# Top-2 expert dispatch: an early store of one row per partition instead of three, and the first group's other four stores with 16 rows each

## The chip, the cores and the metric

The kernel runs on one core of a Trainium2 chip. The metric is the device time of one execution in microseconds; lower is better. The time of the kernel before is the median of three runs. A profiled execution, taken by the hardware profiler, supplies the trace.

## What is computed

```python
batch, seq, hidden, n_experts, k = 16, 1024, 512, 8, 2
...
probs = softmax(router_logits)                       # over the 8 experts
topk_indices = np.argsort(probs, axis=-1)[..., -k:]
topk_probs = np.take_along_axis(probs, topk_indices, axis=-1)
topk_probs = topk_probs / np.sum(topk_probs, axis=-1, keepdims=True)
x_expanded = x[:, :, np.newaxis, :].repeat(k, axis=2)
return (x_expanded * topk_probs[..., np.newaxis]).astype(np.float32)
```

(The first two lines of the softmax are written as one call here.) For each of 16,384 tokens the two largest of 8 router probabilities are scaled to sum to one, and the token's 512 values are written out twice, once times each of the two weights, the smaller first. The output has 67.1 MB, twice the 33.6 MB of `x`.

## The kernel before

**Tiling.** The tokens are cut into two groups. Group 0 has 65 tokens per partition, group 1 has 63, on 128 partitions. A "row" is one token on each partition: 2 KB of `x` per partition going in, 4 KB per partition (two scaled copies) going out. Each group lies so that a partition's tokens are contiguous in memory, so that a load or store of n rows moves one contiguous run per partition.

**Buffers.** `xs` holds 65 rows of `x`. `osp` holds `L = 18` rows of output. There is no room for a whole group of outputs, so half of the stores write their products into `osp`, and the other half write them into parts of `xs` whose input rows are no longer needed (an output row takes two rows of `xs`).

**Loads.** `LOADS` gives the rows of each load: 2, 4, 28 and 31 for group 0, and 16, 16 and 31 for group 1. All are issued by SP at line 122. After the first six rows the two router-logit transfers are issued (lines 130 and 131) and `top2_weights` computes all weights into `WA`: a tournament of maxima and minima on VectorE (lines 26 to 36) and two sigmoids on ScalarE (lines 37 and 38). Its scratch lies in `osp`.

**Stores.** `STORES` lists each store as (first row, rows, buffer, place in the buffer). For each, VectorE multiplies the rows of `xs` with the weights into the place (line 138), then the store is issued (line 151). The very first store of group 0, the early store, is issued by ACT; the rest are issued by SP in program order, after the loads that stand ahead of them in the code. In group 0 these are:

```python
[(0, 3, "osp", 0), (3, 15, "osp", 3), (18, 16, "xs", 0), (34, 15, "osp", 0), (49, 16, "xs", 33)],
```

In this document they are called the early store, store 1, store 2, the third store (store 3) and store 4. Group 1 has four stores of 16, 16, 15 and 16 rows.

**Splitting the third store's product.** A product that goes to place 0 of `osp` again is cut in two (`again`, line numbers just above 138): the first `FREE[g]` rows lie where the early store's rows lay, and need only that store to have landed. The rest lie where store 1's rows lay and need store 1 to have landed. `FREE` is 3 for group 0 and 2 for group 1.

**Order of the work.** Transfers on SP go out in the order of the code: the group's loads, then its stores, then the next group's loads. The scheduler places VectorE's instructions. The loads of group 1 write rows of `xs` that stores 2 and 4 of group 0 read, and wait for these to land; the last, of 31 rows, waits for store 4.

Of the kernel before, what the change touches and what calls it, by code (L numbers as in the profile page):

```python
# [1 line left out]

# [4 lines left out]

F32 = mybir.dt.float32
ALU = mybir.AluOpType
ACTF = mybir.ActivationFunctionType  # L10
P = 128


def top2_weights(nc, WA, dlt, room, logits, E):

    tt = nc.vector.tensor_tensor
    hi, lo, n = None, None, E  # L20
    while n > 1:
        n //= 2
        if hi is None:
            a, b = logits[:, :, 0:n], logits[:, :, n : 2 * n]
            nhi, nlo = room(n), b
            tt(nhi, a, b, op=ALU.max)  # L26
            tt(nlo, a, b, op=ALU.min)  # L27
        else:
            a, b = hi[:, :, 0:n], hi[:, :, n : 2 * n]
            nhi, nlo, tmp = room(n), room(n), room(n)  # L30
            tt(tmp, lo[:, :, 0:n], lo[:, :, n : 2 * n], op=ALU.max)  # L31
            tt(nlo, a, b, op=ALU.min)  # L32
            tt(nlo, nlo, tmp, op=ALU.max)  # L33
            tt(nhi, a, b, op=ALU.max)  # L34
        hi, lo = nhi, nlo
    tt(dlt, hi[:, :, 0], lo[:, :, 0], op=ALU.subtract)  # L36
    nc.scalar.activation(WA[:, :, 0], dlt, ACTF.Sigmoid, scale=-1.0)  # L37
    return nc.scalar.activation(WA[:, :, 1], dlt, ACTF.Sigmoid, scale=1.0)  # L38

GROUPS = [65, 63]

LOADS = [[2, 4, 28, 31], [16, 16, 31]]
BASE = [0, 1]

STORES = [
    [(0, 3, "osp", 0), (3, 15, "osp", 3), (18, 16, "xs", 0), (34, 15, "osp", 0), (49, 16, "xs", 33)],
    [(0, 16, "osp", 2), (16, 16, "xs", 0), (32, 15, "osp", 0), (47, 16, "xs", 32)],
]  # L50

L = 18

FREE = [3, 2]


@with_exitstack
def kernel(
    ctx: ExitStack,
    tc: tile.TileContext,  # L60
    x: bass.AP,
    router_logits: bass.AP,
    k: bass.AP,
    out: bass.AP,
):
    nc = tc.nc
    B, S, D = x.shape
    E = router_logits.shape[-1]
    N = B * S
    assert int(k) == 2 and E == 8 and N == P * sum(GROUPS)  # L70
    M = N // P

    x_v, o_v, rl_v = [], [], []
    t0 = 0
    for n in GROUPS:
        t1 = t0 + P * n
        x_v.append(
            x.rearrange("b s d -> (b s) d")[t0:t1].rearrange("(p m) d -> p m d", p=P)
        )
        o_v.append(  # L80
            out.rearrange("b s k d -> (b s) k d")[t0:t1].rearrange(
                "(p m) k d -> p m k d", p=P
            )
        )
        rl_v.append(
            router_logits.rearrange("b s e -> (b s) e")[t0:t1].rearrange(
                "(p m) e -> p m e", p=P
            )
        )
        t0 = t1  # L90

    wpool = ctx.enter_context(tc.tile_pool(name="wpool", bufs=1))
    xs = wpool.tile([P, max(GROUPS), D], F32)
    osp = wpool.tile([P, L, 2, D], F32)
    WA = wpool.tile([P, M, 2], F32)
    dlt = wpool.tile([P, M], F32)


    flat = osp.rearrange("p l k d -> p (l k d)")
    taken = [0]  # L100

    def room(n):
        o = taken[0]
        taken[0] += M * n
        return flat[:, o : o + M * n].rearrange("p (m n) -> p m n", n=n)

    logits = room(E)

    def place(where, at, n):

        if where == "osp":
            return osp[:, at : at + n]
        return xs[:, at : at + 2 * n, :].rearrange("p (r k) d -> p r k d", k=2)

    moved = []
    m0 = 0
    for g, G in enumerate(GROUPS):
        x0, r = BASE[g], 0
        for n in LOADS[g]:
            moved.append(  # L120
                tc.keep_in_program_order(
                    nc.sync.dma_start(  # L122
                        xs[:, x0 + r : x0 + r + n, :], x_v[g][:, r : r + n, :]
                    )
                )
            )
            r += n
            if g == 0 and r == 6:
                n0 = GROUPS[0]
                tc.keep_in_program_order(nc.sync.dma_start(logits[:, :n0], rl_v[0]))  # L130
                tc.keep_in_program_order(nc.sync.dma_start(logits[:, n0:], rl_v[1]))  # L131
                weights = top2_weights(nc, WA, dlt, room, logits, E)
        assert r == G
        for r, n, where, at in STORES[g]:
            og = place(where, at, n)
            again = where == "osp" and at == 0 and r > 0
            for a, b in [(0, FREE[g]), (FREE[g], n)] if again else [(0, n)]:
                product = nc.vector.tensor_tensor(  # L138
                    og[:, a:b],
                    xs[:, x0 + r + a : x0 + r + b, :]  # L140
                    .unsqueeze(2)
                    .to_broadcast([P, b - a, 2, D]),
                    WA[:, m0 + r + a : m0 + r + b, :]
                    .unsqueeze(3)
                    .to_broadcast([P, b - a, 2, D]),
                    op=ALU.mult,
                )

            queue = nc.scalar if g == r == 0 else nc.sync
            moved.append(  # L150
                tc.keep_in_program_order(queue.dma_start(o_v[g][:, r : r + n], og))  # L151
            )
        m0 += G

    seen = tc.keep_in_program_order(nc.sync.nop())
    for ins in [weights, product] + moved[:-1]:
        tc.add_manual_dep(
            seen.ins,
            ins.ins.name,
            mybir.DependencyInfo(  # L160
                mybir.DependencyClass.Sync, mybir.DependencyReason.DATA
            ),
            reason="all but the last transfer is done",
        )


# [1 line left out]
_INS = ['x', 'router_logits', 'k']  # L168
_OUTS = [((16, 1024, 2, 512), 'float32')]

_NUMBERS = {'k': 2}


# [26 lines left out]
```

## Time and profile before

| what | us |
|---|---|
| median of the three runs | 239.71 (239.63 to 239.90) |
| the profiled execution, its own time | 241.36 |
| its span, first to last instruction | 239.6 |
| VectorE busy | 141.9, 22 instructions |
| ScalarE busy | 1.8 |
| VectorE waiting for loads of `x` (twice) | 47.3 |
| VectorE waiting for stores of `osp` (twice) | 14.8 |

The profile page gives busy time by engine, the span in 40 equal slices with the busy share of the 16 DMA engines in tenths, the DMA queues (q1 is SP's, q10 is ACT's) and the chain of work that ended last. Other views of the same trace give the instructions in order of time, the waits, and the DMA share and GB/s in a stretch that one chooses. "SPq" and "ACTq" are the sequencers that issue transfers. In the view by stretches the columns are the stretch, its length, the busy time and count of VectorE, ScalarE and GpSimd, the clock, the DMA share and GB/s; a packet is counted whole in the stretch in which it starts, so that the share of a short stretch can pass 1.

### The profile page before, as it was taken

To read this page: it belongs to the slowest core of one execution; us is meant where nothing else is said; L and a number is where in the kernel's file an instruction comes from. 1 tells how busy PE (TensorE), PEld (TensorE's weight loads), DVE (VectorE), ACT (ScalarE), POOL (GpSimd) and SP (SyncE) were. 2 spreads that over 40 slices of the span, in tenths; PEclk is the share of its full clock that TensorE was granted. 3 is DMA by queue.
4 is the path that set the end of the run, shared out by engine and by line. 5 is a ranking of instruction groups with operands and counts; after the bars stand their busy time and mean duration, and the time that the engine had idled before them with its cause. 6 is when DMAs were issued, how large, how long until landed. Compare 5 with 4: busy or idle time off the path is not lost.

```text
span 239.6 us, 106 instructions
## 1 busy us (share of the span) xinstructions
DVE 141.9 (59%) x22; ACT 1.8 (1%) x3; POOL 0.2 (0%) x4
## 2 busy tenths in 40 slices
DVE  0560499999789999200000699999405999960000
ACT  2000000000000000000000000000000000000000
POOL 0000000000000000000000000000000000000000
DMA  7989998979989897999899999999999899898984
GB/s 253 528 373 483 427 415 376 493 339 492 481 372 492 383 482 339 482 437 449 361 421 438 438 438 498 435 419 471 405 405 471 372 503 442 380 492 360 514 350 186
DMA packets 2592, 101.19 MB, mean 422 GB/s; under 512 B 288, under 2 KB 416, under 8 KB 672
## 3 DMA queue, kind: packets, MB, share of 16 engines
q1 hardware_dynamic: 2448, 99.62, 96.7%
q10 hardware_dynamic: 144, 1.57, 1.5%
HBM read 34.08 MB, written 67.11 MB: 422 GB/s over the span
## 4 chain that ended last, share of the span: by engine, by line
DMA 48%; DVE 40%; SPq 1%; issue 0%; DVEq 0%
DMA xs<-in_x_dram 25%; DVE osp L138 25%; DMA out_dram<-osp 23%; DVE xs L138 14%; SPq L122 0%; SPq L131 0%; SPq L130 0%; SPq L151 0%; DVEq L138 0%
## 5 line engine op out<-in xcount | busy, mean ns | idle before, releaser
L138 DVE TENSOR_TENSOR osp<-xs,WA 128x3072 f32<-128x3072 f32 (+5 forms) x7 | 69.4, 9909 | 62.7 <-DMA xs<-in_x_dram 47.3
L138 DVE TENSOR_TENSOR xs<-xs,WA 128x16384 f32<-128x16384 f32 x4 | 68.9, 17224 | 0.1
L26 DVE TENSOR_TENSOR osp<-osp 128x512 f32<-128x512 f32 x1 | 0.7, 693 | 8.5 <-DMA osp<-in_router_logits_dram 8.5
L37 ACT ACT_TABLE_LOAD x1 | 1.3, 1283 | 0.7 <-PEq L181 0.7
L27 DVE TENSOR_TENSOR osp<-osp 128x512 f32<-128x512 f32 x1 | 0.7, 691 | 0.0
L32 DVE TENSOR_TENSOR osp<-osp 128x256 f32<-128x256 f32 (+1 forms) x2 | 0.7, 351 | 0.0
L31 DVE TENSOR_TENSOR osp<-osp 128x256 f32<-128x256 f32 (+1 forms) x2 | 0.7, 350 | 0.0
L34 DVE TENSOR_TENSOR osp<-osp 128x256 f32<-128x256 f32 (+1 forms) x2 | 0.7, 350 | 0.0
L33 DVE TENSOR_TENSOR osp<-osp 128x256 f32<-128x256 f32 (+1 forms) x2 | 0.7, 350 | 0.0
L37 ACT ACTIVATE WA<-dlt 128x128 f32<-128x128 f32 x1 | 0.3, 315 | 10.5 <-DVE dlt L36 10.5
L36 DVE TENSOR_TENSOR dlt<-osp 128x128 f32<-128x128 f32 x1 | 0.3, 292 | 0.0
L38 ACT ACTIVATE WA<-dlt 128x128 f32<-128x128 f32 x1 | 0.3, 297 | 0.0
L181 POOL MEMSET const-bfloat16-1.0<- 128x1 bf16 x1 | 0.1, 101 | 0.0
L181 POOL MEMSET const-uint8-127<- 128x1 uint8 x1 | 0.1, 101 | 0.0
L181 POOL MEMSET const-float32-0.0<- 128x1 f32 x1 | 0.1, 98 | 0.2 <-issue 0.2
L181 POOL MEMSET const-float32-1.0<- 128x1 f32 x1 | 0.1, 98 | 0.0
## 6 DMA issues: line engine op xcount, KB each, us to landing
out_dram<-osp SPq DMA_DIRECT2D x3, 7680.0 KB, 23.5
xs<-in_x_dram SPq DMA_DIRECT2D x2, 7936.0 KB, 42.2
xs<-in_x_dram SPq DMA_DIRECT2D x2, 4096.0 KB, 40.1
xs<-in_x_dram SPq DMA_DIRECT2D x1, 7168.0 KB, 24.8
out_dram<-osp ACTq DMA_DIRECT2D x1, 1536.0 KB, 26.6
xs<-in_x_dram SPq DMA_DIRECT2D x1, 1024.0 KB, 5.9
xs<-in_x_dram SPq DMA_DIRECT2D x1, 512.0 KB, 3.9
osp<-in_router_logits_dram SPq DMA_DIRECT2D x1, 260.0 KB, 6.2
```

The source lines that it names most:

```text
L26: tt(nhi, a, b, op=ALU.max)
L27: tt(nlo, a, b, op=ALU.min)
L31: tt(tmp, lo[:, :, 0:n], lo[:, :, n : 2 * n], op=ALU.max)
L32: tt(nlo, a, b, op=ALU.min)
L33: tt(nlo, nlo, tmp, op=ALU.max)
L34: tt(nhi, a, b, op=ALU.max)
L36: tt(dlt, hi[:, :, 0], lo[:, :, 0], op=ALU.subtract)
L37: nc.scalar.activation(WA[:, :, 0], dlt, ACTF.Sigmoid, scale=-1.0)
L38: return nc.scalar.activation(WA[:, :, 1], dlt, ACTF.Sigmoid, scale=1.0)
L138: product = nc.vector.tensor_tensor(og[:, a:b], xs[:, x0 + r + a : x0 + r + b, :] .unsqueeze(2) .to_broadcast([P, b - a, 2, D]), WA[:, m0 ...
L181: nc = _bacc.Bacc("TRN2", target_bir_lowering=False, num_devices=1)
```

## The change

The five stores of group 0 are cut in another way: 1, 16, 16, 16 and 16 rows instead of 3, 15, 16, 15 and 16. Store 1 takes places 1 to 16 of `osp` instead of 3 to 17; the third store takes 16 rows of `osp` instead of 15, and its first part, the rows that need only the early store to have landed, is one row instead of three. Store 4 and group 1 are unchanged, as are all loads.

```diff
 STORES = [
-    [(0, 3, "osp", 0), (3, 15, "osp", 3), (18, 16, "xs", 0), (34, 15, "osp", 0), (49, 16, "xs", 33)],
+    [(0, 1, "osp", 0), (1, 16, "osp", 1), (17, 16, "xs", 0), (33, 16, "osp", 0), (49, 16, "xs", 33)],
     [(0, 16, "osp", 2), (16, 16, "xs", 0), (32, 15, "osp", 0), (47, 16, "xs", 32)],
 ]
...
-FREE = [3, 2]
+FREE = [1, 2]
```

In the built program the number of instructions on each engine is the same. On VectorE the third store's first part, behind the product of store 2 before, now stands ahead of it:

```
before: osp 3 rows | osp 15 | xs 16 | osp 3  | osp 12 | xs 16 | ...
after:  osp 1 row  | osp 16 | osp 1 | xs 16  | osp 15 | xs 16 | ...
```

## The prediction

> **What bounds the kernel now.** I read the page first (busy time, slices, bytes), then the chain of waits, then the timeline around the first four stores, and last the DMA share in short windows there.
>
> ```profile
> span 239.6 us, 106 instructions
> DVE 141.9 (59%) x22; ACT 1.8 (1%) x3; POOL 0.2 (0%) x4
> DMA  7989998979989897999899999999999899898984
> q1 hardware_dynamic: 2448, 99.62, 96.7%
> q10 hardware_dynamic: 144, 1.57, 1.5%
> HBM read 34.08 MB, written 67.11 MB: 422 GB/s over the span
> ```
>
> VectorE works 59% of the span, the two DMA queues (q1 issued by SP, q10 by ACT) 98%. The DMA digits never fall below 7 before the last slice. The bound is the 101.19 MB that must pass; an edit gains only if it fills DMA idle time and loses only if it makes some. The chain shows who hands work to whom:
>
> ```profile
> 2.56 24.83 DMA xs<-in_x_dram
> ...
> 27.42 16.17 DVE osp L138
> ...
> 43.60 23.45 DMA out_dram<-osp
> ...
> 67.08 12.97 DVE osp L138
> ...
> 80.07 17.23 DVE xs L138
> ```
>
> The 28-row load lands at 27.39, its product ends at 43.58, store 1 (15 rows) is issued at 43.60 and lands at 67.05, and only then may the third store's product rewrite `osp`. The chain alternates between DMA and VectorE, but that is order, not idleness: the DMA has other transfers queued all the while. How many is the question here, so I looked at when packets start (bytes of a window are those of packets that start in it):
>
> ```profile
> 44.70:45.50 0.80, 0.80 (x1) 0.00 (x0) 0.00 (x0) 1.00 2.97 1190
> 45.50:47.30 1.80, 1.80 (x1) 0.00 (x0) 0.00 (x0) 1.00 0.10 35
> 47.30:47.90 0.60, 0.60 (x1) 0.00 (x0) 0.00 (x0) 1.00 3.56 1536
> 47.90:48.50 0.60, 0.60 (x1) 0.00 (x0) 0.00 (x0) 1.00 0.00 0
> 48.50:48.60 0.10, 0.10 (x1) 0.00 (x0) 0.00 (x0) 1.00 1.42 614
> 65.40:66.00 0.60, 0.00 (x0) 0.00 (x0) 0.00 (x0) 1.00 3.79 1638
> 66.00:66.60 0.60, 0.00 (x0) 0.00 (x0) 0.00 (x0) 1.00 0.00 0
> 66.60:66.70 0.10, 0.00 (x0) 0.00 (x0) 0.00 (x0) 1.00 1.52 655
> 84.70:85.30 0.60, 0.60 (x1) 0.00 (x0) 0.00 (x0) 1.00 3.56 1536
> 85.90:86.10 0.20, 0.20 (x1) 0.00 (x0) 0.00 (x0) 1.00 0.71 307
> ```
>
> Last column GB/s. 1536 GB/s for 0.6 us is 0.92 MB, or 15 packets of 61,440 B (15 rows of 4 KB, one partition); 614 for 0.1 us is one such packet. So 15 DMA engines start store 1 at 47.3 to 47.9 and one, the straggler, at 48.5. The pattern repeats at store 2 (65.4 to 66.0; 66.6) and store 3 (84.7 to 85.3; about 86): nothing is lost between, and the straggler's lag of 0.6 us is carried along. Each landing waits for the straggler, so **the straggler's idle time is what counts**; the other 15 have 0.6 us or more to give away.
>
> ```profile
> 60.86 0.34 SPq L151 DMA_DIRECT2D out_dram<-xs  x1
> 97.33 0.33 SPq L151 DMA_DIRECT2D out_dram<-xs  x1
> 123.83 0.33 SPq L122 DMA_DIRECT2D xs<-in_x_dram  x1
> SPq L122 <- DMA out_dram<-xs: 24.0, 1, 24.0
> ```
>
> The 31-row load at 123.83 was released by store 4's landing. From 67.05 to 123.8 stores 2, 3 and 4 passed, 47 rows of 524,288 B: 24.64 MB in 56.75 us, 434 GB/s, **1.207 us a row** (16 rows 19.3, 15 rows 18.1).
>
> **The change part by part.** Bytes and transfers stay as many. Group 0's stores go from 3, 15, 16, 15, 16 rows to 1, 16, 16, 16, 16; after the third store both kernels have stored 49 rows.
>
> ```profile
> 13.02 3.36 DVE L138 TENSOR_TENSOR osp<-xs,WA 128x3072 f32<-128x3072 f32 x1 [0.58 <-ACT WA L38]
> 16.40 0.37 ACTq L151 DMA_DIRECT2D out_dram<-osp  x1
> L138 DVE TENSOR_TENSOR osp<-xs,WA 128x16384 f32<-128x16384 f32 x1 | 17.2, 17224 | 36.3 <-DMA xs<-in_x_dram 36.3
> L138 DVE TENSOR_TENSOR osp<-xs,WA 128x15360 f32<-128x15360 f32 x1 | 16.2, 16157 | 11.0 <-DMA xs<-in_x_dram 11.0
> L138 DVE TENSOR_TENSOR osp<-xs,WA 128x2048 f32<-128x2048 f32 x1 | 2.3, 2284 | 0.0
> out_dram<-osp ACTq DMA_DIRECT2D x1, 1536.0 KB, 26.6
> q10 hardware_dynamic: 61, 0.75, 15.9%
> ```
>
> A row costs VectorE 17.22 - 16.16 = 1.07 us, so one row alone takes 2.28 - 1.07 = 1.2.
>
> *Early store.* Its product takes 1.2 instead of 3.36 us, so ACT issues at 14.3 instead of 16.40. It carries 2 rows less: the engines are through with it and the loads 2 x 1.207 = **2.4 us earlier**. The last row, queue q10 between 16 and 27 us, shows 0.75 MB of it moved ahead of the 28-row load's landing. At a third the size and one more turn (16 packets of 4 KB) that is 0.32 MB, 0.43 MB or 1.0 us less; some of the 61 packets went after the load's last data, so I take **0.8 us** (bounds: 0, and 1.7 if all 0.75 MB were gone).
>
> *Store 1, 16 rows.* The product starts 0.8 earlier and takes 1.07 longer: issue at 43.60 + 0.27 = **43.9** (bounds 43.0 and 44.7). The engines are free 2.4 earlier: fifteen at 44.9 to 45.5, the straggler at **46.1**. Before, this gap between issue and need was 48.5 - 43.6 = 4.9 us on the straggler, now 2.2. It must cover the lag L from an issue to its first packet. Nearest row, the very first load on idle queues:
>
> ```profile
> 0.72 0.85 SPq L122 DMA_DIRECT2D xs<-in_x_dram  x2
> 0.00:1.70 1.70, 0.00 (x0) 0.98 (x1) 0.20 (x4) 1.00 0.00 0
> 1.70:2.10 0.40, 0.00 (x0) 0.31 (x1) 0.00 (x0) 1.00 1.37 164
> ```
>
> Issued at 0.72, nothing by 1.7, then 66 KB by 2.1, sixteen packets of 4 KB: L is 1.0 to 1.4 us. The other bound is store 1 before: issued 43.60, running at 47.3 behind the loads, so L is at most 3.7. I take 1.0 to 1.4, because store 1 would now meet the same condition, an engine about to be free; the 3.7 holds time spent behind the loads. Then store 1 is ready at 44.9 to 45.3: a few tenths of waiting on some of the fifteen, **nothing on the straggler**.
>
> *The third store's first row.* Its one-row product now stands ahead of store 2's product on VectorE (in the kernel before, the three-row product at 60.75 stood behind it). It needs the early store's landing: 16.40 + 26.6 = 43.0 before, some 2 us earlier now, against a need at 43.9. Behind it waits store 2's product: 43.9 + 1.2 + 17.2, issue at 62.3 instead of 60.86. The engines need store 2 at 64.2 to 64.8 (44.9 to 45.5 plus 19.3), the straggler at 65.4: 3.1 us for L. Cost 0; without the cover each us costs one.
>
> *Store 3, 16 rows.* Store 1 lands at 65.4 plus 0.4 (67.05 against the straggler's end at 66.65), 65.8; 15 more rows take 16.16, so issue at 82.0 instead of 80.07. Store 2 leaves the engines at 83.5 to 84.1, the straggler at 84.7: 2.7 us for L. Cost 0.
>
> *Store 4 and later.* Issue at 99.3; the straggler is through with 49 rows at 84.7 + 19.3 = 104.0, as before (86.0 + 18.1). Behind store 4 on SP stand the second group's loads, issued 2 us later, into queues full until 123.8. From there nothing differs.
>
> **Sum:** 0. The profiled execution took 241.36 us, 1.8 around its span of 239.6; the runs shown have a median of 239.71. With both unchanged I predict **239.7**.
>
> One rule would move a term. The 61 packets of q10 by 27 us, of 128, and its landing only at 43.0 show it taking turns with the load all along. The Trainium skill, "DMA: Bandwidth & Descriptors", section "Queues, rings and completion order", says each engine drains a whole packet of about 9 to 17 descriptors before it turns to another queue. By that rule the early store's 8 descriptors per engine would pass in one go, and the 28-row load would gain all 2.4 us. The trace disagrees, so 0.8 stays.
>
> **The rivals.**
>
> *Slower: the DMA runs dry at stores 1 and 3.* It decides from L = 2.2 us. At 3.0, store 1 loses 0.8 (46.9); it lands at 66.6, store 3 is issued at 82.8 and ready at 85.8, where the straggler is free at 85.6: together 1.0 us, 240.7. At 3.7: 1.5 at store 1 (47.6), lands 67.3, store 3 ready at 87.2 against 86.3, together 2.4: 242.1. For it: all gaps shrink from nearly 5 us to 2 or 3, and L under load is seen nowhere. Against: the first load's 1.0 to 1.4.
>
> *Slower: the small transfer is slow.* A 512 KB transfer, the first load, needs 3.9 us from issue to landing where 1.2 would do at full rate:
>
> ```profile
> xs<-in_x_dram SPq DMA_DIRECT2D x1, 512.0 KB, 3.9
> q1 hardware_dynamic: 99, 0.43, 106.7%
> ```
>
> If the early store held the engines so, it would cost 2.7: 242.4. Against it the second row, 3 to 4 us into the span: 99 packets of mostly 4 KB, 0.43 MB in 1 us, full rate.
> The Trainium skill, the same page, section "Bandwidth", asks for at least 1 MiB per transfer; the early store falls below that, and by this rule it would lose. The trace shows the fixed part hidden when other packets are queued.
>
> *Faster: the straggler catches up.* Its lag arises in the loads, between which the early store's packets pass. If shorter packets undo it, all later landings come up to 0.6 us earlier: 239.1. Against: nothing shows that those packets cause it.
>
> **How the numbers follow.** Unchanged 0.62, dry 0.28, small transfer 0.03, straggler gone 0.07. Less than 0.2% (0.48 us) is about what a measurement of this kernel can tell from no change. Slower is 0.28 + 0.03 = 0.31, faster 0.07. Range 239.2 to 241.2: it takes in the dry case up to L of about 3.2 and leaves out its worst part, the small transfer and half of the faster case, some 0.15. The likeliest case alone spans 239.4 to 240.1.
>
> **What would show it.** Early store issued at 14.3; store 1's product started at 26.6, its issue at 43.9; store 2 at 62.3; store 3 at 82.0; store 4 at 99.3; store 4's landing (the 31-row load's issue) at 123.8 as before. Wrong, if no packet starts on the straggler for more than a few tenths after 46.1 or 84.7, or if the 31-row load is issued later than 124.3.

## The result and the profile after

| | median us | runs |
|---|---|---|
| before | 239.90 | 11 (239.63 to 241.70) |
| after | 240.93 | 11 (240.32 to 242.49) |

The ratio is 1.0045, with a 95% interval of 1.0026 to 1.0064: the change makes the kernel about 1 us slower. A second set of runs of both gave 1.0047 (1.0025 to 1.0070).

The page of the changed kernel, the rows that answer to those of before:

```profile
span 239.6 us, 107 instructions
DVE 141.8 (59%) x22; ACT 1.8 (1%) x3; POOL 0.2 (0%) x4
DMA  7989898989898989898969999799998989989894
q1 hardware_dynamic: 2448, 100.66, 98.1%
q10 hardware_dynamic: 144, 0.52, 0.5%
```

The 107 instructions against 106 are one more wait of VectorE's sequencer; the instructions that work are as many on each engine. The span is that of the first trace of before, though the median is 1 us higher. The reason lies on the other side: the first trace of before was of an execution that took 241.36 us, 1.6 more than the median of 239.71 (the trace of after was of one that took 241.41, 0.5 more than its median). A second trace of the kernel before, shown below beside the first, has a span of 238.0, and no straggler. The chain of waits of the changed kernel:

```profile
26.11 17.24 DVE osp L138
...
43.36 21.28 DMA out_dram<-osp
...
64.73 16.17 DVE osp L138
...
80.92 17.24 DVE xs L138
```

Store 1's product starts at 26.1, store 1 is issued at 43.4 and lands at 64.6, store 3 is issued at 80.9: each 0.5 to 1.2 us earlier than forecast. Did a queue run empty? The view by stretches of the changed kernel, around the start of store 1 (columns as before, the last are DMA share and GB/s of packets that start in the stretch):

```profile
41.80:42.60 0.80, 0.80 (x1) 0.00 (x0) 0.00 (x0) 1.00 2.93 1270
42.60:44.20 1.60, 1.60 (x2) 0.00 (x0) 0.00 (x0) 1.00 0.00 0
44.20:44.60 0.40, 0.40 (x2) 0.00 (x0) 0.00 (x0) 1.00 4.18 1802
44.60:45.20 0.60, 0.60 (x1) 0.00 (x0) 0.00 (x0) 1.00 1.26 546
```

1270 GB/s for 0.8 us are sixteen packets of 63,488 B, the last of the loads, one on each engine. At 2.34 us each they end at 44.1 to 44.9. Store 1's sixteen packets start at 44.2 to 45.2. The packets' own times show a gap of 0.03 us on one engine and none on the other fifteen, and none at store 3: **the queues did not run dry**. The first packet came 0.86 us after the issue at 43.36.

Where then did the time go? In each stretch the DMA share can be held against the bytes. What the engines were busy beyond what the bytes need at 434 GB/s is the excess: length x (share - GB/s / 434). Behind the first 8 us it is at most some 0.15 us in every other stretch of these four traces, and stands at four places: the end of the 28-row load (between 20 and 26.5 us, where the early store's packets come between the load's), the turn from the loads to store 1 (41 to 46.5), the turn from store 4 to the second group's loads (119 to 124.7) and the turn back to stores (157 to 162.5). First the two traces of before, then the two of after:

```profile
20.00:26.50 6.50, 0.00 (x0) 0.00 (x0) 0.00 (x0) 1.00 1.03 413
119.00:124.70 5.70, 0.00 (x0) 0.00 (x0) 0.00 (x0) 1.00 0.93 402
157.00:162.50 5.50, 5.50 (x1) 0.00 (x0) 0.00 (x0) 1.00 0.88 375
```

```profile
20.00:26.50 6.50, 0.00 (x0) 0.00 (x0) 0.00 (x0) 1.00 0.99 402
119.00:124.70 5.70, 0.00 (x0) 0.00 (x0) 0.00 (x0) 1.00 1.03 443
157.00:162.50 5.50, 5.50 (x1) 0.00 (x0) 0.00 (x0) 1.00 0.90 375
```

```profile
20.00:26.50 6.50, 0.39 (x1) 0.00 (x0) 0.00 (x0) 1.00 1.11 478
119.00:124.70 5.70, 0.00 (x0) 0.00 (x0) 0.00 (x0) 1.00 0.98 368
157.00:162.50 5.50, 5.50 (x1) 0.00 (x0) 0.00 (x0) 1.00 1.05 375
```

```profile
20.00:26.50 6.50, 0.64 (x1) 0.00 (x0) 0.00 (x0) 1.00 1.11 479
119.00:124.70 5.70, 0.00 (x0) 0.00 (x0) 0.00 (x0) 1.00 0.99 368
157.00:162.50 5.50, 5.50 (x1) 0.00 (x0) 0.00 (x0) 1.00 1.00 375
```

Look at the last row of each: always 375 GB/s, so the same bytes, but a share of 0.88 and 0.90 before and of 1.05 and 1.00 after. By the formula the turn at 160 us has an excess of 0.1 and 0.2 us per engine before, 1.0 and 0.75 after; the turn at 122 has 0.0 before, 0.75 and 0.8 after. In exchange the 28-row load's end loses 0.5 and 0.4 before and 0.05 after. So the change gains 0.4 to 0.5 us in the loads and loses about 1.5 at two turns that lie some 80 and 115 us behind store 1's issue, in transfers that are the same in both kernels.

A second sign of a lasting difference is a small one. The two 16-row loads behind store 4 are issued by SP one after the other, and the second issue takes

```profile
98.74 1.00 SPq L122 DMA_DIRECT2D xs<-in_x_dram  x1
```

in the first trace of before and

```profile
99.85 1.24 SPq L122 DMA_DIRECT2D xs<-in_x_dram  x1
```

after (1.05 and 1.24 in the second traces): already at 98 us, long before the first costly turn, something in the DMA differs.

### The profile page after: what moved, and what is told of

The parts are those of the page before. It is cut to its first block, busy times and chain, and to the rows that moved or that the text cites. A ratio compares the mean times of both kernels' runs of the same rounds, so it can differ in the third digit from the quotient of the medians.

```text
span 239.6 us, 107 instructions
## 1 busy us (share of the span) xinstructions
DVE 141.8 (59%) x22; ACT 1.8 (1%) x3; POOL 0.2 (0%) x4
## 4 chain that ended last, share of the span: by engine, by line
DMA 46%; DVE 41%; SPq 1%; issue 0%; DVEq 0%
DVE osp L138 27%; DMA xs<-in_x_dram 24%; DMA out_dram<-osp 22%; DVE xs L138 14%; SPq L122 0%; SPq L131 0%; SPq L130 0%; SPq L151 0%; DVEq L138 0%
## 5 line engine op out<-in xcount | busy, mean ns | idle before, releaser
L138 DVE TENSOR_TENSOR osp<-xs,WA 128x1024 f32<-128x1024 f32 (+4 forms) x7 | 69.3, 9909 | 62.9 <-DMA xs<-in_x_dram 46.9
## 6 DMA issues: line engine op xcount, KB each, us to landing
out_dram<-osp ACTq DMA_DIRECT2D x1, 512.0 KB, 23.8
```

The costliest lines, as they stand in the source:

```text
L138: product = nc.vector.tensor_tensor(og[:, a:b], xs[:, x0 + r + a : x0 + r + b, :] .unsqueeze(2) .to_broadcast([P, b - a, 2, D]), WA[:, m0 ...
```

## The experiments

All are judged by the ratio of their runs to runs of the kernel before on the same chip, and by the excess at the four places. **Lead** of a store is the time from its issue to the start of its first packet. It is how far ahead of need the store was queued, plus the lag of about 0.9 us, where no queue ran dry. By the packets' own times the engines stood idle in one kernel alone, before_store12_later, for 0.4 us on average at store 1; in the others it was under 0.1 us at any store or turn. The excess is a mean over the 16 engines, while the time goes by the slowest of them. Issues come from the timeline, packet starts from the trace's packets. The table has every kernel; the sections say what each was for.

| kernel | lead of stores 1, 2, 3 | excess in the loads (25 + 45 us) | excess at the turns (122 + 160 us) | ratio, 95% interval |
|---|---|---|---|---|
| again_before | 4.1, 5.0, 5.6 | 0.41 + 0.11 | 0.05 + 0.20 | 1.0002 (0.9983 to 1.0022) |
| again_after | 1.1, 2.2, 2.2 | 0.04 + 0.03 | 0.81 + 0.75 | 1.0047 (1.0025 to 1.0070) |
| early2_store1_16 | 1.5, 3.6, 3.8 | 0.22 + 0.00 | 0.43 + 0.84 | 1.0019 (0.9999 to 1.0039) |
| early3_store1_14 | 5.2, 4.8, 4.5 | 0.41 + 0.16 | 0.06 + 0.42 | 0.9993 (0.9979 to 1.0006) |
| early3_store1_16 | 3.0, 1.2, 5.5 | 0.59 + 0.00 | 0.58 + 0.97 | 1.0044 (1.0031 to 1.0058) |
| early1_store1_15 | 1.9, 1.7, 0.9 | 0.06 + 0.03 | 0.87 + 0.80 | 1.0054 (1.0036 to 1.0072) |
| before_later_products | 3.9, 4.7, 3.1 | 0.57 + 0.00 | 0.06 + 0.42 | 1.0000 (0.9987 to 1.0012) |
| after_scalar_helps | 3.0, 4.1, 3.3 | 0.04 + 0.20 | 0.28 + 0.47 | 1.0029 (1.0020 to 1.0038) |
| early2_store1_15 | 3.4, 4.2, 2.9 | 0.16 + 0.54 | 0.17 + 0.25 | 1.0016 (1.0002 to 1.0031) |
| before_19_places | 4.2, 5.0, 5.6 | 0.40 + 0.05 | 0.04 + 0.36 | 1.0006 (0.9994 to 1.0018) |
| early4_store1_14 | 6.3, 5.9, 6.4 | 0.62 + 0.00 | 0.02 + 0.09 | 0.9998 (0.9990 to 1.0007) |
| before_store12_later | 0.8, 1.8, 5.0 | 0.45 + 0.00 | 0.88 + 0.79 | 1.0075 (1.0056 to 1.0095) |
| before_store2_later | 4.0, 1.3, 4.5 | 0.57 + 0.05 | 0.88 + 0.82 | 1.0081 (1.0062 to 1.0101) |
| after_scalar_helps_more | 5.6, 6.7, 5.8 | 0.06 + 0.80 | 0.00 + 0.14 | 1.0010 (0.9998 to 1.0022) |
| before_store3_later | 3.9, 4.7, 1.8 | 0.51 + 0.16 | 0.18 + 0.53 | 1.0050 (1.0035 to 1.0066) |
| after_store2_helped | 0.9, 7.0, 1.9 | 0.06 + 0.03 | 0.81 + 0.86 | 1.0085 (1.0053 to 1.0117) |
| after_scalar_helps_three | 5.1, 6.2, 5.5 | 0.11 + 0.91 | 0.01 + 0.09 | 1.0006 (0.9981 to 1.0032) |
| after_stores23_helped | 1.1, 7.1, 6.4 | 0.04 + 0.03 | 0.75 + 0.80 | 1.0044 (1.0023 to 1.0064) |

### Both kernels once more, and other row counts

The first question was whether the loss at the turns belongs to the changed kernel or to single executions.

> The kernel before, once more, for a second trace of it. Theory 'turn': the DMA engines lose time only where the queues turn between loads and stores (excess of the last packets ahead of a turn over 2.42 us for 65,536 B), and the kernel before loses under 0.5 us per engine at store 4 to load and at the 31-row load to store 5 together, as in its first trace (0.1). Its span should be near 238 us, since its runs of 239.7 lie 1.8 us above the span. Theory 'chance': the turns cost about as much as in the changed kernel (0.7 and 1.0 us) in some executions of either kernel; then this trace may show 1 us or more, and the time is still 1.000 of the other runs of before.

> The changed kernel, once more. Theory 'turn': again 1.5 to 2 us lost per engine at the same two turns, ratio 1.004. Theory 'dry' (a queue runs empty at store 1 or 3 in the executions that the first trace does not show): a gap of 0.5 us or more between the end of the loads and the first packet of store 1 on some engines, or at store 3. Theory 'chance': the loss sits at other turns this time and the ratio is nearer 1.002 or less.

It belongs to the kernel: the second traces repeat it, at the same two turns, and there was no gap at store 1 or 3. "Chance" and "dry" fall. Then the row counts, one part of the change at a time:

```diff
-    [(0, 3, "osp", 0), (3, 15, "osp", 3), (18, 16, "xs", 0), (34, 15, "osp", 0), (49, 16, "xs", 33)],
+    [(0, 2, "osp", 0), (2, 16, "osp", 2), (18, 16, "xs", 0), (34, 15, "osp", 0), (49, 16, "xs", 33)],
...
-FREE = [3, 2]
+FREE = [2, 2]
```

> Early store 2 rows, store 1 16 rows, third store 15 as before. Theory 'turn by size' (the loss comes with 16-row packets in all the stores ahead of the turn): store 3 has 15 rows, so the turns cost as little as before, ratio 1.000. Theory 'turn by early store' (short packets of the early store leave the engines in step, and engines in step pay for the turn together): in between, 1.002. Theory 'dry': gap at store 1 about 1.2 us larger margin than in the changed kernel, ratio 1.000.

Its third store has 15 rows and the loss is there, which speaks against "turn by size". It is weak evidence: the trace is of a run of 241.6 us, while seven of the twelve runs took 239.8 to 240.0 as before, and no trace shows whether those lose anything at the turns.

```diff
+    [(0, 3, "osp", 0), (3, 14, "osp", 3), (17, 16, "xs", 0), (33, 16, "osp", 0), (49, 16, "xs", 33)],
```

> Early store 3 rows as before, store 1 14 rows, third store 16. Theory 'turn by size': store 3 has 16 rows, so the turns cost as after the change, ratio 1.004. Theory 'turn by early store': as before, 1.000. Theory 'dry': store 1 is issued a us earlier, more margin there; store 3 as after the change; ratio 1.000 unless store 3 was the dry one.

No loss at 122 us, and no change of the time: a third store of 16 rows is harmless, so "turn by size" falls. Two theories were left, the early store's rows and store 1's:

```diff
+    [(0, 3, "osp", 0), (3, 16, "osp", 3), (19, 16, "xs", 0), (35, 14, "osp", 0), (49, 16, "xs", 33)],   # L = 19
...
+    [(0, 1, "osp", 0), (1, 15, "osp", 1), (16, 16, "xs", 0), (32, 17, "osp", 0), (49, 16, "xs", 33)],   # FREE = [1, 2]
```

> Early store 3 rows as before, store 1 16 rows (osp with 19 places), third store 14. Theory 'early' (fewer rows in the early store bring the loss at the turns): as before, excess at store 4's end and at the 31-row load's end under 0.5 us together, ratio 1.000. Theory 'store 1' (16 rows in the first store behind the loads bring it): excess 1 us or more, ratio 1.003 to 1.005.

> Early store 1 row as after, store 1 15 rows as before, third store 17 rows (two packets of 34 KB per partition). Theory 'early': loss as after the change, ratio 1.003 to 1.005. Theory 'store 1': none, ratio 1.000.

Both lost, though each theory had named only one. Neither count alone is the cause. Three controls followed:

```diff
+    [(0, 2, "osp", 0), (2, 15, "osp", 2), (17, 16, "xs", 0), (33, 16, "osp", 0), (49, 16, "xs", 33)],   # FREE = [2, 2]
...
+L = 19                                                                                # before, nothing else
...
+    [(0, 4, "osp", 0), (4, 14, "osp", 4), (18, 16, "xs", 0), (34, 15, "osp", 0), (49, 16, "xs", 33)],   # FREE = [4, 2]
```

> Early store 2 rows, store 1 15 rows, third store 16. Theory 'store 1' (16 rows in the first store behind the loads bring the loss): none, ratio 1.000, the second of the two 16-row load issues near 123 us takes about 1.03 us as before. Theory 'early' (under 3 rows): loss, ratio 1.002 to 1.005, and that issue takes 1.24 us. Theory 'build' (each build of the kernel draws a placement of its own, whatever its rows): either.

> The kernel before with 19 places in osp instead of 18, the last unused; the same instructions and transfers. Theories 'early' and 'store 1': ratio 1.000 and excess at the two turns under 0.5 us. Theory 'build': if the place of the small tiles behind osp matters, 1.003 to 1.005, which would also take away the reading of the run with early store 3 and store 1 16 rows.

> Early store 4 rows, store 1 14 rows, the rest as before. Theories 'early' and 'store 1': ratio 1.000, no loss. Theory 'build': about as likely a loss of 1 us as none.

(The load issue that the first of these texts puts near 123 us stands near 98 us.) The first kernel came out between, with 0.4 us at the turns and a ratio of 1.0016. A place more in `osp` does nothing, so a chance of the build is unlikely; and the kernels now stood in the order of something else, the lead of their stores.

### The lead, with every transfer unchanged

A first attempt went before the row counts were settled:

```diff
+            if g == 0 and where == "osp" and r > 0:
+                parts.insert(-1, (parts[-1][0], parts[-1][0] + 2))
```

> The kernel before, whose first two rows of store 1 and of the third store's second part are computed twice: every transfer is the same, and stores 1 to 4 are issued about 2.3 us later, so that store 1 is ready some 2 us ahead of its need instead of 4. Theory 'margin' (transfers that are issued close to their turn bring the loss): loss as after the change, ratio 1.003 or more. Theories 'early' and 'store 1': ratio 1.000, excess at the two turns under 0.5 us.

It missed half of its aim. Store 1's repeated rows had come with the small first loads, so they were computed while VectorE waited for the 28-row load, and stores 1 and 2 kept their lead (3.9 and 4.7 us). Only stores 3 and 4 moved, to leads of 3.1 and 4.0, and no more was lost than with the place added alone.

> The changed kernel, with the last two rows of store 1 and of the third store multiplied on ScalarE (8 instructions of 128x512): every transfer is the same as after the change, and stores 1 to 4 are issued about 2.1 us earlier. Theory 'margin': the loss goes, ratio 1.000 or, as the early part is shorter, 0.998. Theories 'early' and 'store 1': loss as after, ratio 1.004.

Half of the loss at the turns went, though the row counts and transfers are the changed kernel's: the first sign for the lead. The next pair takes the lead away from the kernel before with extra products whose result is not used; `osp` has 19 places for it, and VectorE's products are kept in the order of the code:

```diff
+            if g == 0 and r == 3:          # store 1; in the second kernel r == 18, store 2
+                for i in range(3):
+                    tc.keep_in_program_order(nc.vector.tensor_tensor(
+                        osp[:, 18:19], xs[:, 33:34, :]..., WA[:, 33:34, :]..., op=ALU.mult))
```

> The kernel before with 19 places in osp and three extra one-row products into the spare place ahead of store 1's product, once the 28-row load has landed: every transfer is the same, stores 1 and 2 are issued about 3.4 us later (store 1 about 0.8 us ahead of the first engine's need instead of 4.2, store 2 about 1.6 instead of 5.0), store 3 as before. Theory 'lead' (the later stores 1 and 2 are issued ahead of their need, the more is lost at the turns at 122 and 160 us, though no queue runs empty): excess there 1 us or more, ratio 1.003 to 1.005. Theory 'rows' (the sizes of the early store and store 1 bring it, not the lead): ratio 1.000 as the run with 19 places. Theory 'dry': gap of some tenths at store 1.

> The same three extra products between store 1's and store 2's product: store 1 is issued as before (lead 4.2 us), store 2 about 3.4 us later (lead 1.6). Theory 'lead', with store 2 the one that counts: as the run with both later, 1.003 to 1.005. With store 1 the one that counts, or theory 'rows': ratio 1.000.

The timeline of the kernel with store 2 alone later:

```profile
43.21 0.35 SPq L161 DMA_DIRECT2D out_dram<-osp  x1
64.00 0.34 SPq L161 DMA_DIRECT2D out_dram<-xs  x1
80.14 0.33 SPq L161 DMA_DIRECT2D out_dram<-osp  x1
```

and of the second trace of before:

```profile
42.98 0.35 SPq L151 DMA_DIRECT2D out_dram<-osp  x1
60.24 0.34 SPq L151 DMA_DIRECT2D out_dram<-xs  x1
78.97 0.33 SPq L151 DMA_DIRECT2D out_dram<-osp  x1
```

Stores 1 and 3 stand within 1.2 us of where they were, store 2 is 3.8 us later and still ahead of its need. Its two turns, by stretches:

```profile
119.00:124.70 5.70, 0.00 (x0) 0.00 (x0) 0.00 (x0) 1.00 0.95 345
157.00:162.50 5.50, 5.50 (x1) 0.00 (x0) 0.00 (x0) 1.00 1.01 374
```

Excess 0.9 and 0.8 us, and the time is 0.8% longer. Not a transfer, not a byte differs from before, and extra products that left every lead at 3.1 us or more had cost nothing. **A short lead alone makes the loss.** It is more than the changed kernel's since the 0.6 us in the loads stay, and since by the packets' own times the slowest engine ends 1.0 us behind the mean of the 16 (0.4 in the second traces of before and after). Next the third store, with five extra products ahead of its second part:

> The kernel before with 19 places in osp and five extra one-row products into the spare place ahead of the second part of the third store's product: every transfer is the same, stores 1 and 2 are issued as before (leads 4.2 and 5.0 us), store 3 about 3.5 us later (lead about 2 instead of 5.6) and store 4 as much. Theory 'lead of any store': loss at the turns as in the runs with store 2 later, ratio 1.004 or more. Theory 'lead of store 2': ratio 1.000 as the run with 19 places.

```profile
82.91 0.33 SPq L160 DMA_DIRECT2D out_dram<-osp  x1
100.17 0.33 SPq L160 DMA_DIRECT2D out_dram<-xs  x1
```

```profile
119.00:124.70 5.70, 0.00 (x0) 0.00 (x0) 0.00 (x0) 1.00 0.88 368
157.00:162.50 5.50, 5.50 (x1) 0.00 (x0) 0.00 (x0) 1.00 0.96 375
```

With a lead of 1.8 us at store 3 the excess is 0.2 and 0.5 us, the ratio 1.005. The mean excess is only 0.2 to 0.6 us above that of kernels without loss (0.1 to 0.5 us in all); most of the rest is one engine, which falls from 0.4 to 1.1 us behind the mean at the turn near 160 us. So the loss is not store 2's alone. But store 4 is late here too, at 100.17 us with a lead of 2.6, so that this run does not tell store 3 from store 4. The run with a lead of 3.1 at store 3 (and 4.0 at store 4) had shown nothing.

### The lead given back to the changed kernel

The changed kernel's transfers stay; ScalarE takes over some rows of the products, so that the stores are issued earlier (two rows in the run above, four and three here):

```diff
+            if g == 0 and where == "osp" and r > 0:
+                parts[-1] = (parts[-1][0], n - 4)
+                for i in range(n - 4, n):
+                    for j in range(2):
+                        nc.scalar.activation(og[:, i, j], xs[:, x0 + r + i], ACTF.Copy,
+                                             scale=WA[:, m0 + r + i, j : j + 1])
```

> The changed kernel with the last four rows of store 1 and of the third store on ScalarE: the transfers of the changed kernel, stores 1 and 2 issued about 4.3 us earlier than in it (leads about 5 and 6.3 us). Theory 'lead': the loss goes, ratio 0.998 to 1.001. Theory 'rows': as after the change, 1.003 to 1.005.

> The changed kernel with the last three rows of store 1 and of the third store on ScalarE: leads of about 4.2 us at store 1, 5.4 at store 2 and 4.5 at store 3, between the runs with two and with four rows there. Theory 'shortest lead' (the smallest lead of any store of the first group sets the loss at the two turns, little from about 3 us up): shortest lead 4.2, loss at the two turns under 0.5 us as in the kernel before; with no excess at the 28-row load and 0.1 to 0.5 us at the 31-row load, ratio 0.998 to 1.001. Theory 'rows': 1.004.

The stretches of the run with three rows:

```profile
41.00:46.50 5.50, 5.50 (x2) 0.00 (x0) 0.00 (x0) 1.00 1.03 375
119.00:124.70 5.70, 0.00 (x0) 0.00 (x0) 0.00 (x0) 1.00 0.85 368
157.00:162.50 5.50, 5.50 (x1) 0.00 (x0) 0.00 (x0) 1.00 0.88 375
```

With all leads at 5 us or more, the two late turns cost 0.0 and 0.1 us, as before; the row counts are cleared. But 0.9 us now appears at the turn from the loads to store 1 (share 1.03 against 0.87 for the same 375 GB/s in the changed kernel), so that the time only returns to that of before. The other two runs gave the lead to store 2 alone, and to stores 2 and 3:

> The changed kernel with the first four rows of store 2 multiplied on ScalarE and the third store's first row behind store 2's product: the transfers of the changed kernel, store 1 issued as in it (lead about 1 us), store 2 about 4.5 us earlier (lead 2.1 plus 4.5, 6 to 7 us). Theory 'lead of store 2': the loss at the turns at 122 and 160 us goes, and as the 28-row and 31-row loads of the changed kernel show no excess either, the time falls below that of both kernels, ratio 0.995 to 0.998. Theory 'rows': 1.004 as after the change. If the lead of store 1 counts: 1.002 to 1.004.

> The changed kernel with ScalarE taking the first four rows of store 2 and the last four of the third store, but none of store 1: leads of about 1 us at store 1, 7 at store 2, 6 at store 3. Theory 'shortest lead of any store', store 1 counted: the loss at the turns at 122 and 160 us stays at 1.4 us or more, ratio 1.004 or more. If only stores 2 and 3 count: under 0.3 us lost at the two turns and nothing at the loads, ratio 0.995 to 0.998.

```profile
119.00:124.70 5.70, 0.00 (x0) 0.00 (x0) 0.00 (x0) 1.00 0.98 368
157.00:162.50 5.50, 5.50 (x1) 0.00 (x0) 0.00 (x0) 1.00 1.01 375
```

These rows are of the second: store 1 alone has a short lead, 1.1 us, and the whole loss of the changed kernel is there, 0.75 and 0.8 us, ratio 1.0044. The hope for a time below both kernels fell with it. So store 1 and store 2 each count by themselves, and store 3 at least together with store 4. What orders the excess at the two turns, by one trace of each kernel, is the **shortest lead among stores 1 to 3**: from 3.1 us up the two turns cost 0.1 to 0.5 us together, at 2.9 to 3.0 us 0.4 and 0.75, at 1.8 us 0.7, at 1.5 us and less 1.3 to 1.8. The times follow it less closely: the kernel with the lead given to store 2 alone has a ratio of 1.0085 with no more excess than the changed kernel, and its trace, of a run of 240.81 us against a median of 241.79, does not show why.

## Why the prediction was wrong, point by point

- **The bound.** Right: the DMA was never idle before the end, before or after.
- **Early store and the 28-row load.** Early store issued at 14.26 as forecast (14.3). Store 1's product was to start at 26.6, 0.8 us earlier; it started at 26.1, 1.3 earlier (0.9 between the second traces, 26.80 and 25.86). The term was too small by 0.1 us in the second traces and by 0.5 in the first, where the straggler held the load of before back. It counted only the bytes: the load's own packets lost 0.4 to 0.5 us per engine beside the 12 KB packets, and next to nothing beside 4 KB ones.
- **Issues of the stores.** Forecast 43.9, 62.3, 82.0 and 99.3; measured 43.4, 61.6, 80.9 and 98.2. The order was right; the issues came 0.5, 0.7, 1.1 and 1.1 us earlier, the first by the earlier start of the product, stores 3 and 4 by store 1's landing 1.2 us earlier.
- **The lag.** 1.0 to 1.4 us was taken, the changed kernel shows 0.86 at most. The rival that a queue runs dry did not happen; its price was worked out for an idle time that never came. That the measured 240.93 lies near its 240.7, and inside the range that was widened for it, is luck. The small transfer was not slow either (the excess of the loads around it is 0.1 us), and the early store kept taking turns with the loads: 23.8 us to its landing, not the one go of the Trainium skill's page ("DMA: Bandwidth & Descriptors", section "Queues, rings and completion order").
- **The straggler.** It belonged to the one execution of before that was traced; the second trace of before has none. The profiled run's 241.36 us beside a median of 239.71 said so: with 1.8 us around the span, a median run has a span near 237.9, not 239.6. Reading this would have put the engines' need 1 us earlier, and made "nothing on the straggler" a margin of a few tenths.
- **"From there nothing differs."** This is the step that failed. The sum priced a store that is issued ahead of its need at nothing, however short the lead. The leads after the change were 0.9 to 2.2 us at stores 1 to 3, against 3.7 to 5.6 before. The runs show that a lead under about 3 us brings an excess of up to 1.8 us at turns whose transfers are unchanged, 40 to 115 us later. The changed kernel's landing of store 4 (the issue of the 31-row load, 123.26 and 122.97 us against 123.83 and 123.06) looks like "as before" only because the 0.5 us gained in the loads had just been lost there; the second half of the loss comes at 160 us. So neither of the signs that the prediction named could show it.

## What to carry to other kernels

A transfer that is queued just before it is needed is not free, even where no engine idles: here a store had to be issued some 3 us or more ahead of its first packet (a 64 KB packet takes 2.4), shown for two stores one at a time, or later turns between loads and stores cost up to 1.0 us each. So where a size is traded for a shorter lead, price the lead too, and look at the packets' times at later turns of direction, not only for gaps. And compare the profiled execution's own time with the median before reading tenths of a microsecond out of it.

## What was not expected of the hardware

Between the turns the packets of the stores keep one speed within 2% (65,536 B in 2.42 to 2.47 us on an engine, in every trace). The spread between kernels comes from the four places, 0 to 1.0 us per engine at each, and from how far one engine falls behind the others. What a short lead leaves behind in the DMA, for 40 us and more, is not shown by these runs. It shows itself once on the way: the second 16-row load's issue, between 95 and 102 us, takes 1.2 us or more in every kernel with a lead under 3 us at some store, 1.0 to 1.1 with a shortest lead between 3.1 and 4.5, and 0.72 to 0.91 above 5. For example, in the kernel with store 2 later and in the changed kernel with three rows on ScalarE:

```profile
99.07 1.25 SPq L122 DMA_DIRECT2D xs<-in_x_dram  x1
```

```profile
96.87 0.72 SPq L122 DMA_DIRECT2D xs<-in_x_dram  x1
```

Nor is it explained why every kernel with an early store of three or four rows pays 0.4 to 0.6 us at the end of the 28-row load, whatever its leads, and why the two kernels with an early store of one row and long leads pay 0.8 to 0.9 us at the turn to store 1 instead. A version without either loss was not found.
